# Attention of block 1: the values as loaded operand, two heads at a time, features on rows

## The chip, the cores and the metric

The kernel runs on one core of a Trainium2 chip. The metric is the device time of one execution in microseconds (us), as a median of several. The core has five engines with an instruction stream each: TensorE (PE in the profile; PEld is its weight loading), VectorE (DVE), ScalarE (ACT), GpSimd (POOL) and SyncE (SP, which here issues most DMAs). TensorE multiplies a loaded operand (weights, at most 128x128) by a moving one that streams by, and writes to PSUM; the other engines work on SBUF and, but for GpSimd here, on PSUM.

## The reference, cut to what matters

Two transformer blocks run on 512 tokens of 1024 features. The change lies in the sparse attention of block 1 (8 heads of 64 features in two groups of four that share keys and values). With 8 blocks of 64 keys and room for 16 chosen ones every causal block is chosen, and the window is as long as the sequence, so both fine branches are causal attention with a distance bias over different keys and values:

```python
def nsa_mixer(q, k_cmp, v_cmp, k_slc, v_slc, k_win, v_win, gate, ...):
    ...
    p_c = masked_softmax(s_c, dist_c >= 0)
    o_cmp = jnp.einsum('bgrsn,bngd->bsgrd', p_c.astype(vc.dtype), vc)
    ...
        pr = masked_softmax(s, (dist >= 0)[:, :, None])
        return jnp.einsum('bgrqk,bgqkd->bgrqd', pr.astype(vg.dtype), vg)
    ...
    gates = jax.nn.sigmoid(gate).reshape(B, S, G, R, 3)
    o = gates[..., 0:1] * o_cmp + gates[..., 1:2] * o_slc + gates[..., 2:3] * o_win
    return o.reshape(B, S, H * dv)

def first_block(x, p, ...):
        ...
        g_a, g_b = jnp.split(jax.nn.sigmoid(gmix), 2, axis=-1)
        mixed = (g_a * (ya @ w_a2d[i]) + g_b * (yb @ w_b2d[i])) @ w_o[i]
```

## The kernel before

Large products are made in a form of float32 with fewer bits (fp32r): each operand is split into a high half, rounded by a ScalarE copy, and a low half, which VectorE gets by subtraction, and three matmuls (`whi`, `wlo` are the halves of the weights) give one product. The weights come by SP's queue into three buffers `raw` and are split there. Some small products are made in plain float32, where the program's one matmul runs as two instructions.

The attention of block 1 is `nsa_tile(qt)` (L981) for the four query tiles of 128 tokens. Tile qt looks at W = 128(qt+1) keys. It first makes the compressed branch for all 8 heads (L985 to L1012). Then for branch `br` and head `h` it calls `attend` (L957): two matmuls make the scores (PSUM tile `sc`), one VectorE reduction adds the bias into the SBUF tile `P` and finds the extremum, ScalarE takes the exponential in place and sums it, TensorE transposes `P` 128 columns at a time (L968) into the PSUM tile `tp`, ScalarE (L229) and VectorE (L974) copy it in turn into `PT`, and plain float32 matmuls with the 128x128 pieces of `PT` as loaded operand and 64 columns of the values `VT` as moving one add up the output in `pv`, query tokens on rows. There are 64 such heads in all. `P` has three buffers, `PT` two, each PSUM tag two. After the 8 heads of a branch VectorE takes reciprocals of the sums, multiplies by the gate and adds the branch to `o0` (L1025 to L1029). At the end of the tile 4 transpositions bring `o0` to features on rows (`tr4`, L711), and it is split into `yb`.

TensorE has a filler beside this: `gmix` (L914), which makes the gates of the mixture, 16 chunks of 24 matmuls, and then `ya @ w_a2d`, 8 chunks of 12 (rows `mm<-u,whi` and `mm<-a,whi`, 512 columns each). `gmix.run(0.55 * (qt + 1))` per head releases so much of it. A scheduler that knows estimated durations then sets the order of the whole program, and every engine runs its instructions in that order. After the four tiles `gmix.flush()` (L1045) stands, and then the projection of `yb` (L1051). `scan_step` (L916) and `scan_out` (L948), ahead of the tiles, belong to the other mixer of the block; its states lie in `Sst`. Block 2 has an attention of its own by the same `attend` (L1304), which the change leaves.

Of the kernel before, what the change touches and what calls it, by code (L numbers as in the profile page):

```python
# [6 lines left out]
F32 = mybir.dt.float32  # L7
# [185 lines left out]
def body(tc, nc, A, dbg=None, upto=99):  # L193
# [13 lines left out]
    def sb(pool, shape, dt=F32, tag=None, bufs=1):  # L207
        if tag is None:
            nx[0] += 1
            return pool.tile(list(shape), dt, name=f"n{nx[0]}", bufs=bufs)  # L210
        return pool.tile(list(shape), dt, name=tag, tag=tag, bufs=bufs)

    def unit(tag, dt=F32):
        return sb(base, [128, 4, 512], dt, tag, {"u": 4, "a": 11}[tag])
# [41 lines left out]
    ident = cst  # L256
# [248 lines left out]
    gn05 = sb(pA, [128, 1])  # L505

    NG = A["gcst"].shape[1]
    gc0, gc = unit("a").rearrange("p a b -> p (a b)")[:, :NG], sb(pA, [128, NG], F32R)
    POOL.dma_start(gc0, A["gcst"])
    act(gc, gc0, AF.Copy)  # L510
    GR = {k: gc[:, a:b] for k, (a, b) in GCST.items()}
# [5 lines left out]


    U = {nm: unit("a") for nm in "kqv"}
    KV = unit("a")  # L520
    VT = KV[:, 2:4].rearrange("p a b -> p (a b)").rearrange("p (k c) -> p k c", k=4)
    Sst = [r4(KV[:, 0]), r4(KV[:, 1])]
    sm = sb(pA, [128, QT, 32])
    so = outs4(0, 288)
    tout(u, range(8), so, width=288, per=3, tail=3)
    for qt in range(QT):
        DVE.tensor_copy(sm[:, qt], so[qt][:, 256:])
        act(VT[:, qt], so[qt][:, :256], AF.Copy)
    beta, hb, az, gg, ngb = (sb(pA, [128, QT, 4]) for _ in range(5))
    gate = sb(pA, [128, QT, 24])  # L530
    tt(gg, sm[:, :, 4:8], bc(dtb[:, None, :], [128, QT, 4]), ALU.add)
# [74 lines left out]
            yield from fout_g(r, u)  # L606
            qsplit(r[0], QS[0][:, t], QS[1][:, t], 0.125 * 2.0 ** (t + 1), 0.125 * 2.0 ** (t + 5))

    ZF = sb(pA, [128, 4, 512])

    def z_gates():

# [300 lines left out]

    gmix = Fill(gates())  # L914

    def scan_step(c):  # L916
        Sc, Sn = Sst[c % 2], Sst[(c + 1) % 2]
        ut = r4(u0[:, c])
        if c:
            up = ps("sc", B4)  # L920
            for h in range(4):
                mm(up[:, h], r4(wT[:, c])[:, h], Sc[:, h])
            tt(ut, ut, up, ALU.add)
        if c < QT - 1:
            sp_ = ps("tp", B4)
            for h in range(4):
                mm(sp_[:, h], r4(kn[:, c])[:, h], ut[:, h])
            if c:
                tt(Sn, Sc, b4(glast[:, c]), ALU.mult, POOL)
                tt(Sn, Sn, sp_, ALU.add)  # L930
            else:
                DVE.tensor_copy(Sn, sp_)
        op_ = ps("pv", B4)
        for h in range(4):
            if c:
                mm(op_[:, h], r4(qdF[:, c])[:, h], Sc[:, h], start=True, stop=False)
            mm(op_[:, h], r4(qkT[:, c])[:, h], ut[:, h], start=c == 0, stop=True)
        jk = sb(p1, [128, 8, 64], F32, "o0", 2).rearrange("p (h a) d -> p h (a d)", h=4)
        act(jk, op_, AF.Square, scale=128.0 ** -0.5)
        ms = stat(4)  # L940
        DVE.tensor_reduce(ms, jk, axis=AX.X, op=ALU.add)
        tt(ms, ms, rq2[:, c], ALU.mult)
        ts(ms, ms, EPS, None, ALU.add)
        POOL.tensor_tensor(ms, ms, mhalf[:, :4], op=ALU.pow)
        tt(ms, ms, rqk[:, 1, c], ALU.mult)
        tt(ut, op_, b4(ms), ALU.mult)
# [34 lines left out]
    def nsa_tile(qt):  # L981
# [4 lines left out]
        for h in range(8):  # L986
            g, r = divmod(h, 4)
            mm(cs[:, h].rearrange("p a n -> p (a n)"), N["QS"][g][:, r, tok(qt)], N["kc"][:, g].rearrange("p a n -> p (a n)"))
        cp = sb(p1, [128, 2, 8, 32], F32, "cp", 1)
        m8, s8 = stat(8), stat(8)  # L990
        c0 = cp[:, 0]
        tt(c0, cs[:, :, 0], bc(C["bc"][:, None, 32 * qt:32 * qt + 32], [128, 8, 32]), ALU.add)
# [5 lines left out]
        DVE.tensor_reduce(s8, c0, axis=AX.X, op=ALU.add)  # L998
        DVE.reciprocal(s8, s8)
        stt(s8, s8, C["rowok"][:, qt:qt + 1], gq[:, :, 0], ALU.mult, ALU.mult)  # L1000
        b = ps("tp", [128, 2, 128])
        for g in range(2):
            PE.transpose(b[:, g], c0[:, 4 * g:4 * g + 4].rearrange("p r n -> p (r n)"), ident)
        c1 = cp[:, 1].rearrange("p a b -> p (a b)").rearrange("p (g q) -> p g q", g=2)
        act(c1, b, AF.Copy)
        oc = ps("tp", [128, 8, 64])
        for g in range(2):
            mm(oc[:, 4 * g:4 * g + 4].rearrange("p r d -> p (r d)"), c1[:, g], N["VB"][:, g].rearrange("p r d -> p (r d)"))
        o0 = sb(p1, [128, 8, 64], F32, "o0", 2)
        tt(o0, oc, b8(s8), ALU.mult)  # L1010

        nd = C["nd"][:, (3 - qt) * 128:]  # L1012
        for br in range(2):
            acc, sums = ps("pv", [128, 8, 64]), stat(8)
            for h in range(8):
                g, r = divmod(h, 4)

                def score(o):
                    mm(o, N["QS"][g][:, r, tok(qt)], N["K1"][:, 2 * br + g, :W], start=True, stop=False)
                    mm(o, N["QS"][g][:, r, tok(qt)], N["KL"][:, 2 * br + g, :W], start=False, stop=True)  # L1020

                gmix.run(0.55 * (qt + 1))
                attend(p1, score, W, qt, lambda k: VT[:, k, br * 128 + g * 64:br * 128 + g * 64 + 64], acc[:, h],
                       sums[:, h:h + 1], nd, 2.0 ** -(h + 1))
            DVE.reciprocal(sums, sums)  # L1025
            tt(sums, sums, gq[:, :, 1 + br], ALU.mult)
            o1 = sb(p1, [128, 8, 64], F32, "o1", 1)
            tt(o1, acc, b8(sums), ALU.mult)
            tt(o0, o0, o1, ALU.add)  # L1029
        show(f"yb{qt}", o0)  # L1030
        b = tr4(o0.rearrange("p (j h) d -> p j (h d)", j=4), None, "tp")
        split(yb.h[0][:, :, tok(qt)], yb.l[0][:, :, tok(qt)], b)

    gmix.run(5)
    for c in range(QT):
# [349 lines left out]
```

## Time and profile before

| | us |
|---|---|
| median of 3 runs (lowest to highest) | 1559.28 (1555.16 to 1561.36) |
| the profiled execution's own time | 1559.06 |
| its span, first to last instruction | 1557.2 |
| TensorE busy (share of the span) | 1508.4 (97%) |
| VectorE busy | 857.8 (55%) |
| ScalarE busy | 639.7 (41%) |
| GpSimd busy | 97.5 (6%) |
| mean granted TensorE clock | 0.989 |

The tiles of `nsa_tile` run from about 270 to 468 us of the span. Busy is the union of an engine's instructions; a busy TensorE is not one at its peak, since matmuls are pipelined and their ends are modelled. The granted clock is given as a share of 2.4 GHz, of which 0.5 is the lower level.

### The profile page before, as it was taken

To read this page: it belongs to the slowest core of one execution; us is meant where nothing else is said; L and a number is where in the kernel's file an instruction comes from. 1 tells how busy PE (TensorE), PEld (TensorE's weight loads), DVE (VectorE), ACT (ScalarE), POOL (GpSimd) and SP (SyncE) were. 2 spreads that over 40 slices of the span, in tenths; PEclk is the share of its full clock that TensorE was granted. 3 is DMA by queue.
4 is the path that set the end of the run, shared out by engine and by line. 5 is a ranking of instruction groups with operands and counts; after the bars stand their busy time and mean duration, and the time that the engine had idled before them with its cause. 6 is when DMAs were issued, how large, how long until landed. Compare 5 with 4: busy or idle time off the path is not lost.

```text
span 1557.2 us, 19391 instructions
## 1 busy us (share of the span) xinstructions
PE 1508.4 (97%) x7512; PEld 1268.7 (81%) x7512; DVE 857.8 (55%) x1422; ACT 639.7 (41%) x1165; POOL 97.5 (6%) x163
## 2 busy tenths in 40 slices
PE   7998999999999999999999999999999999999997
PEld 6886888888877888888888878888878888888886
DVE  5778754556647555666565376789844333333232
ACT  5443553345524344444455354255643222232122
POOL 2012001000000110000011010020110000000000
PEclk9999999999999999999999999999899999999999
DMA  6314211211044053333389551264341233323331
GB/s 212 95 54 149 68 55 55 68 41 41 1 162 149 30 163 95 96 95 101 115 318 353 207 177 41 84 227 136 108 163 41 95 98 103 97 95 95 95 96 67
DMA packets 49051, 176.80 MB, mean 114 GB/s; under 512 B 5688, under 2 KB 5688, under 8 KB 48960
## 3 DMA queue, kind: packets, MB, share of 16 engines
q1 hardware_dynamic: 39168, 140.13, 27.5%
q0 software_dynamic: 9792, 35.43, 6.6%
q8 instruction: 59, 0.97, 0.2%
q14 instruction: 32, 0.26, 0.0%
HBM read 161.89 MB, written 16.27 MB: 114 GB/s over the span
## 4 chain that ended last, share of the span: by engine, by line
PE 90%; DVE 4%; DMA 2%; ACT 2%; issue 1%; POOL 0%; SPq 0%; POOLq 0%; DVEq 0%; ACTq 0%
PE mm L241 35%; PE sc L241 18%; PE pv L241 18%; PE tp L241 17%; PE tp L968 2%; DMA raw<-W 1%; DVE a L232 1%; ACT a L229 1%; PE tp L467 1%; DMA x<-x 1%; DMA a<-low 0%; DVE n L238 0%; PE tp L711 0%; DVE o L232 0%; DVE P L963 0%
## 5 line engine op out<-in xcount | busy, mean ns | idle before, releaser
L232 DVE TENSOR_TENSOR wlo<-raw,whi 128x1024 fp32r<-128x1024 f32 (+1 forms) x194 | 236.8, 1220 | 322.1 <-ACT whi L229 321.5
L229 ACT ACTIVATE whi<-raw 128x1024 fp32r<-128x1024 f32 (+1 forms) x208 | 219.6, 1056 | 425.4 <-PE mm L241 117.0
L241 PE MATMUL mm<-a,whi 128*128 128x512 f32 x608 | 192.0, 394 | 1.1 <-ACT a L229 1.1
L241 PE MATMUL mm<-u,whi 128*128 128x512 f32 x544 | 175.9, 400 | 0.0
L241 PE MATMUL pv<-a,whi 128*128 128x512 f32 (+2 forms) x576 | 160.2, 362 | 1.8 <-ACT a L229 1.2
L241 PEld LDWEIGHTS mm<-a,whi 128*128 128x128 f32 x608 | 113.5, 189 | 24.4 <-ACT a L229 1.4
L241 PEld LDWEIGHTS pv<-a,whi 128*128 128x128 f32 x576 | 104.2, 189 | 18.9 <-ACT a L229 2.1
L241 PE MATMUL mm<-a,wlo 128*128 128x512 f32 x304 | 119.1, 392 | 0.0
L241 PEld LDWEIGHTS mm<-u,whi 128*128 128x128 f32 x544 | 101.3, 190 | 19.6
L241 PE MATMUL tp<-a,whi 128*128 128x512 f32 x368 | 113.8, 390 | 0.0
L241 PE MATMUL mm<-u,wlo 128*128 128x512 f32 x272 | 107.9, 397 | 0.0
L241 PE MATMUL sc<-a,whi 128*128 128x512 f32 x336 | 104.2, 390 | 0.0
L241 PE MATMUL pv<-a,wlo 128*128 128x512 f32 (+2 forms) x288 | 103.7, 361 | 0.0
L238 DVE SCALAR_TENSOR_TENSOR n<-n,n,n 128x511 f32<-128x511 f32 (+23 forms) x120 | 85.0, 733 | 4.8 <-ACT n L229 2.8
L241 PEld LDWEIGHTS tp<-a,whi 128*128 128x128 f32 x368 | 69.1, 188 | 14.3
L241 PE MATMUL sc<-a 128*128 128x128 f32 (+4 forms) x288 | 73.0, 352 | 3.1 <-DVE st L963 3.0
L241 PEld LDWEIGHTS sc<-a,whi 128*128 128x128 f32 x336 | 63.3, 188 | 13.0
L241 PEld LDWEIGHTS pv<-a,PT 128*128 128x128 f32 x480 | 65.3, 196 | 9.3 <-ACT PT L229 4.6
L241 PE MATMUL tp<-a,wlo 128*128 128x512 f32 x184 | 71.6, 389 | 0.0
L241 PE MATMUL pv<-a,PT 128*128 128x64 f32 x480 | 65.4, 272 | 4.3 <-ACT PT L229 3.2
L241 PEld LDWEIGHTS mm<-a,wlo 128*128 128x128 f32 x304 | 57.3, 188 | 11.7
L241 PE MATMUL sc<-a,wlo 128*128 128x512 f32 x168 | 65.4, 389 | 0.0
(351 smaller groups left out, 2732.1 us busy)
## 6 DMA issues: line engine op xcount, KB each, us to landing
raw<-W SPq DMA_DIRECT2D x234, 512.0 KB, 3.6
a<-W SPq DMA_DIRECT2D x22, 512.0 KB, 6.6
low<-a POOLq DMA_DIRECT2D x22, 512.0 KB, 6.7
wlo<-low POOLq DMA_DIRECT2D x14, 512.0 KB, 3.9
w<-rows POOLq DMA_DIRECT2D x7, 512.0 KB, 8.7
a<-low POOLq DMA_DIRECT2D x7, 512.0 KB, 4.7
bd<-bd POOLq DMA_DIRECT2D x8, 320.0 KB, 6.6
x<-x SPq DMA_DIRECT2D x4, 512.0 KB, 9.3
```

The costliest lines, as they stand in the source:

```text
L229: return ACT.activation(out, in_, f, **k)
L232: return (e or DVE).tensor_tensor(out, a, b, op=op)
L238: return DVE.scalar_tensor_tensor(out, a, s, b, op0=op0, op1=op1)
L241: return PE.matmul(out, lhsT=l, rhs=r, start=start, stop=stop, **k)
L467: PE.transpose(b[:, j, :], src[:, k * 128:(k + 1) * 128], ident)
L968: PE.transpose(b[:, k * 128:(k + 1) * 128], p_[:, k * 128:(k + 1) * 128], ident)
```

## The change

Numerators are divided by their sum and multiplied by the gate before they are transposed (GpSimd multiplies `P` by a factor per row that VectorE makes), and the transposed numerators of two heads stand side by side in `PT`, split into halves, for each head by a ScalarE copy and a VectorE subtraction. The values `VT` are kept as 64 high and 64 low columns, which are loaded together, and 256 columns of `PT` (2 heads by 128 tokens) stream by: the output has features on rows (64 of the high part of the values, 64 of the low part), two instructions per key tile, branch and pair of heads, both branches into the same PSUM tile. Four VectorE additions per group of heads bring the two parts into `y`, where the compressed branch, made in the same layout, already lies. The transposition at the end of a tile goes away. For space the scan's states move to buffers of `P`, the compressed branch's `cp` to the constants' buffer `gc`, and `PT` of branch 0 to the buffer of `ZF` (named `zp`); `PT` of either branch has one buffer. `attend` stays for block 2.

```diff
--- before.py
+++ after.py
@@ -505,7 +505,7 @@
     gn05 = sb(pA, [128, 1])
 
     NG = A["gcst"].shape[1]
-    gc0, gc = unit("a").rearrange("p a b -> p (a b)")[:, :NG], sb(pA, [128, NG], F32R)
+    gc0, gc = unit("a").rearrange("p a b -> p (a b)")[:, :NG], sb(pA, [128, NG], F32R, "gc")
     POOL.dma_start(gc0, A["gcst"])
     act(gc, gc0, AF.Copy)
     GR = {k: gc[:, a:b] for k, (a, b) in GCST.items()}
@@ -517,15 +517,15 @@
 
 
     U = {nm: unit("a") for nm in "kqv"}
-    KV = unit("a")
-    VT = KV[:, 2:4].rearrange("p a b -> p (a b)").rearrange("p (k c) -> p k c", k=4)
-    Sst = [r4(KV[:, 0]), r4(KV[:, 1])]
+
+    VT = unit("a", F32R).rearrange("p k (b d) -> p k b d", b=4)
     sm = sb(pA, [128, QT, 32])
     so = outs4(0, 288)
     tout(u, range(8), so, width=288, per=3, tail=3)
     for qt in range(QT):
         DVE.tensor_copy(sm[:, qt], so[qt][:, 256:])
-        act(VT[:, qt], so[qt][:, :256], AF.Copy)
+        v = so[qt][:, :256].rearrange("p (b d) -> p b d", b=4)
+        split(VT[:, qt, :, :64], VT[:, qt, :, 64:], v)
     beta, hb, az, gg, ngb = (sb(pA, [128, QT, 4]) for _ in range(5))
     gate = sb(pA, [128, QT, 24])
     tt(gg, sm[:, :, 4:8], bc(dtb[:, None, :], [128, QT, 4]), ALU.add)
@@ -606,7 +606,7 @@
             yield from fout_g(r, u)
             qsplit(r[0], QS[0][:, t], QS[1][:, t], 0.125 * 2.0 ** (t + 1), 0.125 * 2.0 ** (t + 5))
 
-    ZF = sb(pA, [128, 4, 512])
+    ZF = sb(pA, [128, 4, 512], F32R, "zp").bitcast(F32)
 
     def z_gates():
 
@@ -913,8 +913,11 @@
 
     gmix = Fill(gates())
 
+    state, NP = [None], 3
+
     def scan_step(c):
-        Sc, Sn = Sst[c % 2], Sst[(c + 1) % 2]
+        Sc, Sn = state[0], r4(sb(p1, [128, 512], F32, "P", NP)) if c < QT - 1 else None
+        state[0] = Sn
         ut = r4(u0[:, c])
         if c:
             up = ps("sc", B4)
@@ -986,7 +989,7 @@
         for h in range(8):
             g, r = divmod(h, 4)
             mm(cs[:, h].rearrange("p a n -> p (a n)"), N["QS"][g][:, r, tok(qt)], N["kc"][:, g].rearrange("p a n -> p (a n)"))
-        cp = sb(p1, [128, 2, 8, 32], F32, "cp", 1)
+        cp = sb(pA, [128, NG], F32R, "gc").bitcast(F32)[:, :512].rearrange("p (i h n) -> p i h n", i=2, h=8)
         m8, s8 = stat(8), stat(8)
         c0 = cp[:, 0]
         tt(c0, cs[:, :, 0], bc(C["bc"][:, None, 32 * qt:32 * qt + 32], [128, 8, 32]), ALU.add)
@@ -998,38 +1001,55 @@
         DVE.tensor_reduce(s8, c0, axis=AX.X, op=ALU.add)
         DVE.reciprocal(s8, s8)
         stt(s8, s8, C["rowok"][:, qt:qt + 1], gq[:, :, 0], ALU.mult, ALU.mult)
+        tt(c0, c0, bc(s8[:, :, None], [128, 8, 32]), ALU.mult)
         b = ps("tp", [128, 2, 128])
         for g in range(2):
             PE.transpose(b[:, g], c0[:, 4 * g:4 * g + 4].rearrange("p r n -> p (r n)"), ident)
         c1 = cp[:, 1].rearrange("p a b -> p (a b)").rearrange("p (g q) -> p g q", g=2)
         act(c1, b, AF.Copy)
-        oc = ps("tp", [128, 8, 64])
+        oc = ps("tp", B4)
+        for j in range(4):
+            g, i = divmod(j, 2)
+            mm(oc[:, j], N["VB"][:, g, 2 * i:2 * i + 2].rearrange("p r d -> p (r d)"), c1[:, g])
+
+        y = sb(p1, [128, 8, 64], F32, "o0", 2).rearrange("p (j a) d -> p j (a d)", j=4)
+        act(y, oc, AF.Copy)
+
+        nd = C["nd"][:, (3 - qt) * 128:]
         for g in range(2):
-            mm(oc[:, 4 * g:4 * g + 4].rearrange("p r d -> p (r d)"), c1[:, g], N["VB"][:, g].rearrange("p r d -> p (r d)"))
-        o0 = sb(p1, [128, 8, 64], F32, "o0", 2)
-        tt(o0, oc, b8(s8), ALU.mult)
-
-        nd = C["nd"][:, (3 - qt) * 128:]
-        for br in range(2):
-            acc, sums = ps("pv", [128, 8, 64]), stat(8)
-            for h in range(8):
-                g, r = divmod(h, 4)
-
-                def score(o):
-                    mm(o, N["QS"][g][:, r, tok(qt)], N["K1"][:, 2 * br + g, :W], start=True, stop=False)
-                    mm(o, N["QS"][g][:, r, tok(qt)], N["KL"][:, 2 * br + g, :W], start=False, stop=True)
-
-                gmix.run(0.55 * (qt + 1))
-                attend(p1, score, W, qt, lambda k: VT[:, k, br * 128 + g * 64:br * 128 + g * 64 + 64], acc[:, h],
-                       sums[:, h:h + 1], nd, 2.0 ** -(h + 1))
-            DVE.reciprocal(sums, sums)
-            tt(sums, sums, gq[:, :, 1 + br], ALU.mult)
-            o1 = sb(p1, [128, 8, 64], F32, "o1", 1)
-            tt(o1, acc, b8(sums), ALU.mult)
-            tt(o0, o0, o1, ALU.add)
-        show(f"yb{qt}", o0)
-        b = tr4(o0.rearrange("p (j h) d -> p j (h d)", j=4), None, "tp")
-        split(yb.h[0][:, :, tok(qt)], yb.l[0][:, :, tok(qt)], b)
+            acc = ps("pv", [128, 2, 2, 128])
+            for i in range(2):
+                for br in range(2):
+                    PT = (sb(p1, [128, 4, 512], F32R, "PT", 1) if br else sb(pA, [128, 4, 512], F32R, "zp"))
+                    PT = PT.rearrange("p a b -> p (a b)").rearrange("p (s k r q) -> p s k r q", s=2, k=4, r=2)
+                    for r in range(2):
+                        h = 4 * g + 2 * i + r
+                        gmix.run(0.55 * (qt + 1))
+                        sc = ps("sc")
+                        mm(sc[:, :W], N["QS"][g][:, 2 * i + r, tok(qt)], N["K1"][:, 2 * br + g, :W], start=True, stop=False)
+                        mm(sc[:, :W], N["QS"][g][:, 2 * i + r, tok(qt)], N["KL"][:, 2 * br + g, :W], start=False, stop=True)
+                        p_ = sb(p1, [128, 512], F32, "P", NP)[:, :W]
+                        mn, sm_ = stat(), stat()
+                        DVE.tensor_tensor_reduce(out=p_, in0=sc[:, :W], in1=nd, scale=-2.0 ** -(h + 1), scalar=3e38,
+                                                 op0=ALU.add, op1=ALU.min, accum_out=mn)
+                        act(p_, p_, AF.Exp, scale=-1.0, bias=mn, accum_out=sm_)
+                        DVE.reciprocal(sm_, sm_)
+                        tt(sm_, sm_, gq[:, h, 1 + br:2 + br], ALU.mult)
+                        tt(p_, p_, bc(sm_, [128, W]), ALU.mult, POOL)
+                        b = ps("tp", B4)
+                        for k in range(qt + 1):
+                            PE.transpose(b[:, k], p_[:, k * 128:(k + 1) * 128], ident)
+                        split(PT[:, 0, :qt + 1, r], PT[:, 1, :qt + 1, r], b[:, :qt + 1])
+                    for k in range(qt + 1):
+                        for s_ in range(2):
+                            mm(acc[:, i], VT[:, k, 2 * br + g], PT[:, s_, k], start=br + k + s_ == 0,
+                               stop=br == 1 and k == qt and s_ == 1)
+            for r in range(2):
+                yr = y[64 * r:64 * r + 64, 2 * g:2 * g + 2]
+                for part in (acc[0:64], acc[64:128]):
+                    tt(yr, part[:, :, r], yr, ALU.add)
+        show(f"yb{qt}", y)
+        split(yb.h[0][:, :, tok(qt)], yb.l[0][:, :, tok(qt)], y)
 
     gmix.run(5)
     for c in range(QT):
```

On TensorE, the end of the attention: the rows from the last of the filler (`mm<-a,wlo`) to the first matmul of the projection of `yb` (the last row). Names are output, then the moving and the loaded operand; `n_63` is the identity of the transpositions. Before:

```order
L241 MATMUL mm<-a,wlo 128x512
L241 MATMUL pv<-a,PT 128x64 x4
L968 MATMUL tp<-n_63,P 128x128 x2
L241 MATMUL pv<-a,PT 128x64 x4
L968 MATMUL tp<-n_63,P 128x128 x2
L241 MATMUL pv<-a,PT 128x64 x4
L711 MATMUL tp<-n_63,o_3660 128x128 x4
L241 MATMUL mm<-a,whi 128x512
```

And now. Between the last filler matmul and the first of these rows stand, left out here, the scores of three heads, the products of one pair (`pv<-zp,a`, 8) and the transpositions of one head:

```order
L241 MATMUL pv<-PT,a 128x256
L241 MATMUL sc<-a 128x512
L241 MATMUL sc<-n_1376,a 128x512
L241 MATMUL pv<-PT,a 128x256 x7
L1041 MATMUL tp<-n_63,P 128x128 x8
L241 MATMUL pv<-zp,a 128x256
L1041 MATMUL tp<-n_63,P 128x128 x4
L241 MATMUL pv<-zp,a 128x256 x7
L1041 MATMUL tp<-n_63,P 128x128 x4
L241 MATMUL pv<-PT,a 128x256 x8
L241 MATMUL mm<-a,whi 128x512
```

The scores of four heads, the transpositions of five and the products of four pairs (32 instructions) now stand behind the last filler matmul, where 12 products and 8 transpositions stood.

On VectorE, inside tile 2 (W = 384), where the filler is silent. `L963` is the reduction of the scores with its reading of the accumulator (now `L1033`). Before:

```order
L963 ISA P,st<-sc,n_199 128x384
L963 ISA st 128x1
L974 COPY PT<-tp 128x384
L963 ISA P,st<-sc,n_199 128x384
L963 ISA st 128x1
```

Now:

```order
L232 TENSOR_TENSOR zp<-tp,zp 128x3x128
L1033 ISA P,st<-sc,n_199 128x384
L1033 ISA st 128x1
L1036 RECIPROCAL st<-st 128x1
L232 TENSOR_TENSOR st<-st,n_336 128x1
L232 TENSOR_TENSOR PT<-tp,PT 128x3x128
L1036 RECIPROCAL st<-st 128x1
L1033 ISA P,st<-sc,n_199 128x384
L1033 ISA st 128x1
L232 TENSOR_TENSOR st<-st,n_336 128x1
```

Each head now brings five instructions to VectorE where two heads brought five: the low half stands where every second head had a copy, and a reciprocal and a product of 128x1 for each have come in between.

## Rows read from the trace of the kernel before

**Rows 1.** The page's chain that ended last, shares of the span by engine.
```profile
PE 90%; DVE 4%; DMA 2%; ACT 2%; issue 1%; POOL 0%; SPq 0%; POOLq 0%; DVEq 0%; ACTq 0%
```

**Rows 2.** Stretches: length, engines' busy us, then granted clock, DMA share, GB/s.
```profile
318.14:334.27 16.13, 13.56 (x85) 11.75 (x83) 12.14 (x47) 9.67 (x34) 0.00 (x0) 0.82 0.11 34
334.27:364.88 30.61, 30.61 (x172) 26.49 (x171) 10.40 (x31) 11.23 (x30) 0.00 (x0) 0.98 0.16 52
364.88:421.49 56.61, 51.77 (x400) 47.43 (x399) 41.91 (x120) 34.03 (x89) 0.00 (x0) 1.00 0.04 10
421.49:460.79 39.30, 39.30 (x198) 32.96 (x197) 14.33 (x24) 10.99 (x19) 3.25 (x6) 1.00 0.39 138
460.79:468.33 7.54, 4.02 (x34) 3.43 (x32) 4.50 (x6) 2.56 (x3) 0.00 (x0) 1.00 0.37 119
```

**Rows 3.** The chain of waits, 410 to 470 us: start, duration, what.
```profile
418.16 0.84 PE pv L241 x8
419.00 0.44 PE tp L968 x4
419.44 0.46 PE sc L241 x2
...
421.65 10.91 PE mm L241 x48
...
461.84 1.24 DVE wlo L232
...
463.10 3.62 DMA raw<-W
```

**Rows 4.** Timeline of TensorE near 346 us: start, duration, instruction.
```profile
346.15 0.28 PE L241 MATMUL sc<-n,a 128*128 128x256 f32 x1
346.27 0.28 PE L241 MATMUL sc<-a 128*128 128x256 f32 x1
```

**Rows 5.** VectorE's groups by shape, 270 to 462 us: total, mean ns.
```profile
L963 DVE CUSTOM_DVE_ANT_0 P<-sc,n 128x512 f32<-128x512 f32 x16 | 10.9, 683 | 3.6 <-PE sc L241 1.5 <-PE tp L968 1.1 <-ACT P L229 1.0
L963 DVE CUSTOM_DVE_ANT_0 P<-sc,n 128x384 f32<-128x384 f32 x16 | 8.7, 549 | 2.9 <-PE tp L968 1.5 <-ACT P L229 0.8 <-PE sc L241 0.7
...
L963 DVE DVE_READ_ACCUMULATOR2_ANT st<- 128x1 f32 x64 | 5.3, 83 | 0.0
...
L974 DVE COPY PT<-tp 128x384 f32<-128x384 f32 x8 | 4.5, 556 | 1.8 <-PE tp L968 1.8
...
L1025 DVE RECIPROCAL st<-st 128x8 f32<-128x8 f32 x8 | 1.6, 201 | 2.2 <-ACT P L229 2.2
```

**Rows 6.** VectorE's groups by shape, the whole span, two small shapes.
```profile
L232 DVE TENSOR_TENSOR a<-sc,dm 64x256 f32<-64x256 f32 x12 | 5.0, 420 | 0.7 <-PE sc L241 0.5
L238 DVE SCALAR_TENSOR_TENSOR st<-st 128x1 f32<-128x1 f32 x32 | 5.0, 156 | 29.3 <-ACT t L229 27.3 <-ACT at L229 1.9
```

**Rows 7.** ScalarE's groups by shape, 270 to 462 us.
```profile
L229 ACT ACTIVATION_READ_ACCUMULATOR P<-P,st 128x1 f32 x64 | 12.0, 188 | 0.0
...
L229 ACT ACTIVATE P<-P,st 128x384 f32<-128x384 f32 x16 | 9.8, 614 | 6.0 <-DVE st L963 5.9
...
L229 ACT ACTIVATE PT<-tp 128x384 f32<-128x384 f32 x8 | 3.9, 483 | 3.3 <-PE tp L968 3.3
```

**Rows 8.** GpSimd's groups by shape, the whole span, a product of 128x512.
```profile
L232 POOL TENSOR_TENSOR h<-a,n 128x512 f32<-128x512 f32 x4 | 4.3, 1069 | 3.6 <-DVE a L232 3.6
```

**Rows 9.** Timeline of GpSimd near 252 us (VectorE splits weights beside it).
```profile
252.32 1.95 POOL L232 TENSOR_TENSOR a<-a,n 128x512 f32<-128x512 f32 x1 [8.63 <-DVE a L932]
```

**Rows 10.** Timeline of VectorE near 241 us (GpSimd multiplies from 241.21 on).
```profile
241.26 1.53 DVE L232 TENSOR_TENSOR h<-a,n 128x512 f32<-128x512 f32 x1
```

**Rows 11.** Stretches of 4 us around the end of tile 0, as rows 2.
```profile
326.00:330.00 4.00, 2.19 (x14) 1.86 (x14) 3.96 (x14) 1.07 (x3) 0.00 (x0) 0.82 0.00 0
330.00:334.00 4.00, 3.83 (x14) 3.07 (x13) 1.53 (x6) 2.95 (x10) 0.00 (x0) 0.50 0.02 4
334.00:338.00 4.00, 4.00 (x18) 3.31 (x17) 0.68 (x3) 0.98 (x3) 0.00 (x0) 0.83 0.00 0
```

## Prediction

> **What bounds the kernel now.** I read the chain of waits first. Over the whole span 90% of the chain that ends last is TensorE [rows 1], so time is won only by shortening TensorE's work or filling its gaps, and lost wherever another engine becomes later than TensorE. Then I cut the touched part (block 1's attention, 270 to 468 us) at the places where the filler (the 512-column matmuls of the gates, which depend on nothing in the attention) starts and stops. [rows 2] gives the stretches after the first: A1 (318.14 to 334.27, no filler, end of query tile 0 and start of tile 1), A2 (filler of 4 gate chunks), A3 (364.88 to 421.49, no filler, end of tile 1, all of tile 2, start of tile 3), A4 (filler again) and the tail. A0, before them, is filled. The reader is to see that TensorE is busy for all of A2 and A4, while in A1, A3 and the tail it has 2.57, 4.84 and 3.52 us of gaps, with VectorE at 75%, 74% and 60%. So the filled stretches are bound by TensorE, and the unfilled ones by the interplay of score, reduction, exponential, transposition and copy per head, where VectorE is already close. The rest of the kernel is untouched but for one subtraction per key tile near 60 us, beside TensorE work, and counts nothing.
>
> **The change part by part.** *TensorE.* Before, each of the 160 products of 128 numerators by 64 values is two instructions, and 8 of them take 0.84 us [rows 3], 0.105 each: 320 x 0.105 = 33.6 us. After, 160 instructions of 256 columns do it. Matmuls of that width start 0.12 us apart (346.15 and 346.27 in [rows 4]), though those read other operands; 160 x 0.12 = 19.2, so 14.4 are saved. The 16 transposes at the ends of the tiles go as well, at 0.11 (4 in 0.44, [rows 3]): 1.8. In sum TensorE loses 16.2 us of work.
>
> *VectorE.* Per head the copy of the transposed numerators went to ScalarE or VectorE in turn. Now every head takes a ScalarE copy and a VectorE subtraction from the transposition's PSUM tile. No such subtraction stands in the trace; I take the PSUM copy of the same shape, 0.556 at 384 columns [rows 5], and 0.134 less or more per 128 columns (the step from 0.549 to 0.683 in [rows 5]). Further, per head, a reciprocal and a product on 128x1, at about 0.16 each ([rows 6] has 0.156 for such a shape; the 0.201 of 128x8 in [rows 5] is the upper bound), and per tile 8 additions of 64x256 at 0.420 [rows 6] where before two of 128x512 per branch stood. *GpSimd* multiplies the numerators by the gate over the sum, 1.07 us for 128x512 when alone [rows 8]. This stands between the exponential and the transposition: each head's chain grows by reciprocal, product, GpSimd multiply and crossings, some 1.5 us, which costs nothing as long as three P buffers hold enough heads in flight. The X loads now queue behind these multiplies on GpSimd's queue; they are wanted only after the gates' and yb's projections, whose weight loads alone take 3.62 us each [rows 3], so I cost that at nothing; without this cover it would be some us in the stage after.
>
> *Stretch by stretch* (the filler chunks in each stretch are the same before and after: the order shows 8, 4 and 2 gate chunks, then 8 of 12).
> A0: when the eighth chunk ends, after has 3 heads transposed, 6 scored and none multiplied by values, against 5, 8 and 3. That is 2 x 0.11 + 2 x 0.24 + 3 x 0.21 = 1.3 less: -1.3, deferred into A1.
> A1: VectorE now has 13 reductions with their reads (5.2), 13 low halves at 0.29 (3.7), 8 additions (3.4), 22 small ones (3.5), a compression step (3.3) and a weight split (1.2): 20.3. Such sums overstate: for the 120 instructions of A3 before I get 48.4 in the same way, and the union of their spans is 41.91 [rows 2], 0.86 of it. So 17.5 busy. Over 16.13 us this doesn't fit. At 95% dense it takes 18.4 (+2.3), at 80% 21.9 (+5.8, taken, since VectorE had 75% before with TensorE as a second limit), and with the small ones slower at 75% 24.8 (+8.6).
> A2: TensorE-bound. 96 matmuls at 0.227 (48 in 10.91, [rows 3]) are 21.8; compression 0.9, 14 transpositions 1.5, 5 pairs of scores 1.2, 8 products 1.0: 26.3 against 30.61: -4.3.
> A3: VectorE has 28 reductions (17.6), 29 low halves (15.5), 16 additions (6.7), 51 small ones (8.1), two compressions (6.7) and a split (1.2): 55.8, times 0.86 is 48.1. At 90% dense 53.4 (-3), at 80% 60.1 (+3.7, taken), at 75% with GpSimd in the way 68.5 (+12). ScalarE needs 0.614 + 0.188 + 0.483 = 1.29 us a head of 384 columns [rows 7], below VectorE's 1.5 (0.549 + 0.083 + 0.556 + 0.32), so it isn't the bound.
> A4: 144 filler matmuls 32.7, 24 products 2.9, 7 heads' transpositions 3.1, 4 pairs of scores at 0.46 [rows 3] 1.8: 40.5 against 39.30: +1.2.
> Tail: in the order before, 12 products and 8 transpositions are left after the last filler matmul, 2.1 us of TensorE work in 7.54. After, four heads are still to be scored, five to be transposed and 32 products to be made: 4 x 0.46 + 20 x 0.11 + 32 x 0.12 = 7.9 us of TensorE work, with nothing to fill. By the chain, three heads at VectorE's 512-column pace (0.683 + 0.083 + 0.69 + 0.32 = 1.8) are 5.3, and the last head's way is score 0.5, reduction 0.8, exponential 0.9, gate over sum 0.3, GpSimd 1.1, transposition 0.4, halves 1.3, products 1.0, additions 1.7, last halves 0.6: 8.6. With crossings, and the wait for a weight load of 3.62 and its split of 1.24 [rows 3] that now stand in the middle of this on VectorE, 16 to 18.5. I take 17: +9.5, with +6 if heads overlap at ScalarE's pace, and +11 at most.
> Net: -1.3 + 5.8 - 4.3 + 3.7 + 1.2 + 9.5 = +14.6 on the profiled run's 1559.06 (span 1557.2 and 1.9 around it; it stands 0.2 under the median, so nothing is rescaled): 1573.7, I say 1573. All low ends give -1.3 + 2.3 - 4.3 - 3 + 1.2 + 6 = +0.9, 1560; all high ends +27, 1586.
>
> *A rule against the change.* At 241.26 a VectorE product of 128x512 from two SBUF tensors took 1.53 us beside a GpSimd multiply [rows 10], where such a width takes about 0.69; a GpSimd multiply took 1.95 beside a weight split [rows 9] instead of 1.07 [rows 8]. Both directions enter the last rival below. The Trainium skill's GPSIMD Engine Reference, section Key points, says that GpSimd shares its SBUF interfaces with VectorE and contends with instructions there that have two SBUF inputs; the trace agrees. By the rule, the halves (one input in PSUM) would be spared and the 64 gate products not.
>
> **The rivals.** (a) The forecast: VectorE sets the unfilled stretches and the tail grows by what no longer stands under filler, 1573. (b) A wash: three P buffers let VectorE run dense and the low ends hold, 1560 to 1562. For it speaks that VectorE never waits for GpSimd's product directly; against it that its order alternates reductions and low halves of different heads, so a late head stops those behind it. (c) The other side: VectorE, ScalarE and GpSimd hide under TensorE and all of the 16.2 us is kept, 1543. It decides from the point where A3 ends within some 51 us, VectorE 94% dense, and the tail stays near 7.5; the 7.9 us of TensorE work left there speak against it, the full TensorE of A2 and A4 for a part. (d) Something slower on top. In [rows 11] TensorE was busy for 2.19 of 4 us, the granted clock fell to 0.82 and then 0.50 (the 1.2 GHz level) for 3.83 us of work, then 0.83. Against full clock that is about 0.4 + 1.9 + 0.7 = 3 us a time. A thinner TensorE in A1, at the tile changes in A3 and in the tail could meet this up to three times, +3 to +9; A3 now is at 1.00 throughout [rows 2], which speaks against it. Or contention: 25 gate products in A3, four in ten beside a GpSimd multiply, at 0.84 each, +8. Together with (a) some 1582 to 1590. The Trainium skill's TensorE: Matmul & The Clock Gate, Part 1, says that the clock is gated by how busy the array recently was; the rows agree.
>
> **How the numbers follow.** Chances: (a) 0.50, (b) 0.24, (c) 0.10, (d) 0.16. A measurement of this kernel tells some 0.5% from no change, 7.8 us: (c) is faster, (b) and a small part of (a) the same, the rest slower: 0.10, 0.28, 0.62. The range is 1556 to 1590: it leaves out (c) and the far ends. (a) alone has 1565 to 1582.
>
> **What would show it.** Right: the time from the start of A1 to the start of A2 longer by 2 to 9 us, A2 shorter by about 4, A3 with VectorE at 80% or more and the idle time of TensorE before transpositions released by GpSimd or VectorE, 16 us or so between the last gate matmul and yb's first projection. Wrong: products of 256 columns far from 0.12 us, low halves slower than 0.56 at 384 columns, a tail under 10 us, a clock under 0.9 in A3, or a difference outside 240 to 470 us.

## The result and the profile after

The changed kernel takes 1570.1 us (median of 5 runs, 1567.79 to 1571.69) against 1559.28; the ratio is 1.0073 with an interval of 1.006 to 1.0085. It is slower by 10.8 us, inside the range and on the side that was forecast, 2.9 under the forecast of 1573. One of e3's ten runs below took 1838.03 us at a granted clock of 0.77 and is left out where e3 is compared.

The same stretches, cut where the filler stops and starts (columns as in [rows 2]):

```profile
315.56:336.45 20.89, 16.73 (x70) 13.08 (x68) 17.59 (x83) 12.15 (x44) 4.41 (x11) 0.62 0.09 26
336.45:365.18 28.73, 28.73 (x138) 24.16 (x137) 12.99 (x40) 11.37 (x30) 6.06 (x10) 0.92 0.17 55
365.18:420.43 55.25, 43.46 (x260) 33.32 (x258) 49.80 (x178) 36.16 (x95) 23.03 (x28) 0.97 0.03 11
420.43:461.25 40.82, 40.82 (x204) 34.31 (x205) 23.37 (x48) 16.07 (x29) 6.82 (x7) 1.00 0.21 65
461.25:480.45 19.20, 11.59 (x61) 8.90 (x59) 12.85 (x30) 9.58 (x17) 7.25 (x10) 0.83 0.48 160
```

| stretch | before | forecast | after | difference |
|---|---|---|---|---|
| A0, from the filler block ahead of it (243.57, after 242.26) | 74.57 | -1.3 | 73.30 | -1.3 |
| A1, no filler | 16.13 | +5.8 | 20.89 | +4.8 |
| A2, filler | 30.61 | -4.3 | 28.73 | -1.9 |
| A3, no filler | 56.61 | +3.7 | 55.25 | -1.4 |
| A4, filler | 39.30 | +1.2 | 40.82 | +1.5 |
| tail | 7.54 | +9.5 | 19.20 | +11.7 |
| sum | | +14.6 | | +13.4 |

The profiled execution came 1.3 us earlier to this part than the one of before, and took 1.0 less behind it, so the spans differ by 11.1 (1568.3 and 1557.2). The loss is in A1, a little of it in A4 and, above all, in the tail.

The prices of the new operations, from VectorE's and then GpSimd's groups by line and shape between 270 and 478 us (total us, mean ns of one, idle time before):

```profile
L232 DVE TENSOR_TENSOR st<-st,n 128x1 f32<-128x1 f32 x64 | 14.6, 229 | 1.2
L232 DVE TENSOR_TENSOR o<-pv,o 64x256 f32<-64x256 f32 x29 | 12.2, 420 | 1.9 <-PE pv L241 1.3
L1036 DVE RECIPROCAL st<-st 128x1 f32<-128x1 f32 x64 | 10.1, 158 | 3.1 <-ACT P L229 2.3
L232 DVE TENSOR_TENSOR PT<-tp,PT 128x384 fp32r<-128x384 f32 x8 | 4.4, 552 | 0.0
```

```profile
L232 POOL TENSOR_TENSOR P<-P,st 128x512 f32<-128x512 f32 x16 | 16.5, 1040 | 49.4 <-DVE st L232 30.9 <-DVE st L1036 16.1 <-PE pv L241 2.4
L232 POOL TENSOR_TENSOR P<-P,st 128x384 f32<-128x384 f32 x16 | 13.7, 861 | 15.2 <-DVE st L1036 7.2 <-DVE st L232 4.9 <-ACT PT L229 2.1
```

Low halves, additions and reciprocals came as priced. The gate product took 229 ns on average instead of 160.

The chain of waits through the tail (start, duration, what), to be read against 461.84 and 463.10 in [rows 3]:

```profile
462.83 1.14 DVE wlo L232
463.97 0.45 DVE P L1033
...
464.66 0.59 DVE PT L232
465.25 0.60 DVE P L1033
...
466.09 1.05 POOL P L232
...
468.69 1.53 DVE a L232
...
470.24 3.47 DMA raw<-W
...
473.73 1.07 ACT a L229
...
474.82 1.23 DVE a L232
476.04 0.61 DVE PT L232
...
476.70 1.25 PE pv L241 x7
```

The `a` rows here are no numerators: they are splits of `w_o`'s weights for the stage behind the projection of `yb`. They stand in the in-order queues of ScalarE and VectorE ahead of the last heads' halves. VectorE's split at 468.69 frees the buffer into which the next chunk comes, ScalarE waits 3.47 us for that, and only behind ScalarE's and VectorE's split comes the last low half (476.04). From 468.69 to 476.04 the chain holds no step of a head. It is the path that ended last and not the price of the weights, for the last head's own steps ran beside it:

```profile
471.70 1.04 POOL L232 TENSOR_TENSOR P<-P,st 128x512 f32<-128x512 f32 x1 [2.58 <-DVE st L232]
```

```profile
474.69 0.58 ACT L229 ACTIVATE PT<-tp 128x512 fp32r<-128x512 f32 x1
```

ScalarE's copy (second fence) was done at 475.27, so the last low half waited some 0.7 us more for the split. Four additions and the last high half follow, up to 480.45.

### The profile page after: what moved, and what is told of

It reads as the page before. It is cut to its first block, busy times and chain, and to the rows that moved or that the text cites. A ratio compares the mean times of both kernels' runs of the same rounds, so it can differ in the third digit from the quotient of the medians.

```text
span 1568.3 us, 19433 instructions
## 1 busy us (share of the span) xinstructions
PE 1508.8 (96%) x7352; PEld 1259.5 (80%) x7352; DVE 891.9 (57%) x1586; ACT 654.6 (42%) x1201; POOL 144.1 (9%) x227
## 4 chain that ended last, share of the span: by engine, by line
PE 88%; DVE 6%; ACT 2%; issue 1%; DMA 1%; POOL 1%; SPq 0%; POOLq 0%; DVEq 0%; ACTq 0%
PE mm L241 35%; PE sc L241 18%; PE pv L241 16%; PE tp L241 16%; DVE a L232 1%; DVE P L1033 1%; ACT a L229 1%; DVE o L232 1%; PE tp L971 1%; PE tp L467 1%; PE tp L1041 1%; DMA raw<-W 0%; DMA x<-x 0%; PE tp L711 0%; DVE n L238 0%
## 5 line engine op out<-in xcount | busy, mean ns | idle before, releaser
L241 PE MATMUL sc<-a 128*128 128x512 f32 (+4 forms) x264 | 71.2, 362 | 4.1 <-DVE st L1033 3.1
L448 POOL TENSOR_TENSOR st<-st,n 128x1 f32<-128x1 f32 x32 | 19.3, 603 | 580.1 <-DVE st L238 580.1
L241 PEld LDWEIGHTS mm<-a,wlo 128*128 128x128 f32 x304 | 57.2, 188 | 11.7
L229 ACT ACTIVATE P<-P,st 128x128 f32<-128x128 f32 (+3 forms) x96 | 53.8, 562 | 20.8 <-DVE st L1033 15.5
```

Source lines behind the costliest of these rows:

```text
L229: return ACT.activation(out, in_, f, **k)
L241: return PE.matmul(out, lhsT=l, rhs=r, start=start, stop=stop, **k)
L448: POOL.tensor_tensor(r, r, mhalf[:, 0:1], op=ALU.pow)
```

## The experiments

A stretch is cut as above in each; times of single runs are given without an interval. The part behind the tail, which none of these edits but e10's touches, is up to 3.1 us longer in their profiled executions than in the changed kernel's, so totals of single runs say less than their stretches.

**Less work for VectorE.** e1 takes the normalisation out:

```diff
-                        DVE.reciprocal(sm_, sm_)
-                        tt(sm_, sm_, gq[:, h, 1 + br:2 + br], ALU.mult)
-                        tt(p_, p_, bc(sm_, [128, W]), ALU.mult, POOL)
```

> The changed kernel without the reciprocal, the gate product and GpSimd's multiply of each of the 64 heads (the numerators go to the transposition undivided, so the output lacks the division and the gate of both fine branches). It takes 64 x (0.158 + 0.229) = 24.8 us of instructions from VectorE and one engine from each head's chain. If VectorE's total load sets the unfilled stretches: A1 20.9 -> about 17, A3 55.3 -> about 48, tail 19.2 -> about 17, time 1555 to 1558. If the tail is set by what lost its cover and by the weight load of 3.5 us in the middle of it, A3 shrinks but the tail stays at 16 or more: 1558 to 1564. If the half clock of A1 (granted 0.62) is what costs there, A1 stays above 19.5.

One run took 1568.96, 1.1 less than the changed kernel. A1 19.22, A3 55.02, tail 20.37. Neither of the first two readings holds, and A1 is a little under the 19.5 of the third. VectorE was busy for 42.43 us in A3 instead of 49.80, and the stretch lasted as long. The rows say where it went (A3, then two pieces of 4 us out of it):

```profile
363.01:418.03 55.02, 47.14 (x263) 36.65 (x262) 42.43 (x122) 36.50 (x96) 0.00 (x0) 0.88 0.03 10
```

```profile
379.00:383.00 4.00, 3.32 (x15) 2.52 (x14) 0.95 (x3) 1.71 (x6) 0.00 (x0) 0.50 0.00 0
...
407.00:411.00 4.00, 2.85 (x9) 2.16 (x10) 2.07 (x5) 1.75 (x4) 0.00 (x0) 0.50 0.00 0
```

Both lie at the changes to tiles 2 and 3, where TensorE has little to do while VectorE makes the compressed branch: it was busy for 2.50 and 3.03 of the 4 us ahead of them. The granted clock was at 1.2 GHz there, and A3 as a whole at 0.88 instead of 0.97.

e2 takes the low halves out, with TensorE's work kept:

```diff
-                        split(PT[:, 0, :qt + 1, r], PT[:, 1, :qt + 1, r], b[:, :qt + 1])
+                        act(PT[:, 0, :qt + 1, r], b[:, :qt + 1], AF.Copy)
-                            mm(acc[:, i], VT[:, k, 2 * br + g], PT[:, s_, k], ...
+                            mm(acc[:, i], VT[:, k, 2 * br + g], PT[:, 0, k], ...
```

> The changed kernel without the low halves of the transposed numerators: VectorE's 64 subtractions are left out and the products read the high half twice, so TensorE's work is the same and VectorE loses 31 us of instructions. If VectorE's load sets the unfilled stretches: A1 20.9 -> about 17, A3 55.3 -> 45 to 48, tail 19.2 -> 16 or so, time 1553 to 1558. If the tail's missing cover is the main price, the tail stays at 15 or more and keeps most of the loss: 1558 to 1563. If the clock costs in A1, A1 stays above 19.5 with a clock under 0.7.

1560.14. A1 19.96 (granted 0.61), A3 49.93, tail 17.05. The low halves are worth 10 us, half of it in A3 (which stays over the 45 to 48 of the first reading) and 2.2 in the tail; most of the tail's growth stays without them. A1 hardly moved, as the reading by the clock had it.

**The clock.** e5 keeps TensorE busy in tile 0 with matmuls whose results are overwritten:

```diff
+                        for _ in range(2 if qt == 0 else 0):
+                            mm(sc, N["QS"][g][:, 2 * i + r, tok(qt)], N["K1"][:, 2 * br + g])
                         mm(sc[:, :W], ...
```

> The changed kernel with two more matmuls of 512 columns ahead of the scores of each of tile 0's 16 heads, into the same PSUM tile, which the scores then overwrite; some 20 of the 32 fall into A1, 4.6 us at full clock. If the half clock (0.62 granted in A1, from 320 to 340 us) is what lengthens A1, the clock stays near full, A1 goes from 20.9 to 16 to 19 and A2 starts at full clock (28.7 -> 26.5 to 27.5), although TensorE has more to do: 1564 to 1569 with the 2.8 us that A0 gains. If VectorE's 17.6 us of work set A1, it stays at 20.5 or more whatever the clock is: 1572 or more. If the clock falls all the same, A1 grows by 5 to 9 us.

1574.27; A0 grew by 4.7 (242.50 to 320.46). A1 took 19.12 and A2 28.15. The projection of `yb` begins only 1.1 us later than in the changed kernel; 3.1 us of the longer time lie behind the tail. The clock was at 1.00 up to 335 us, but two reductions fewer were left for A1 (11 instead of 13). Within it VectorE was as dense as at half clock:

```profile
320.46:339.58 19.12, 15.93 (x88) 12.85 (x87) 16.03 (x74) 11.80 (x40) 5.23 (x11) 0.89 0.09 29
```

16.03 of 19.12 is 84%, and 17.59 of 20.89 in the changed kernel is 84% as well. So full clock alone did not make A1 denser; what it took off goes with the two heads. e9 does e2 and e5 together (diffs as there).

> e2_no_low (no low halves of the numerators) together with the two extra matmuls per head of tile 0 that the scores overwrite. Either one alone shortened A1 by 1 to 2 us. If VectorE's work and the half clock of TensorE bound A1 side by side, both together bring A1 to 14 to 16.5 us and the clock there above 0.85; if neither does and it is the order of the heads, A1 stays at 18 or more. Time 1560 to 1566 (the extra matmuls cost A0 some 3 to 5 us).

1562.1, A1 18.11 with a clock of 0.95: below the three others (20.89, 19.96, 19.12), but not the 14 to 16.5 that two bounds side by side would have given. VectorE was busy for 13.88 us of it, 77%, and in the kernel before for 12.14 of 16.13, 75%, with as many heads left (11): at about the same share, the difference is its work. What holds it at that share stays open; the longer way of each head is a candidate that no run here isolates.

e11 repeats e1 with TensorE kept busy at the tile changes:

```diff
-        b = ps("tp", [128, 2, 128])
+        bw = ps("tp")
+        b = bw[:, :256].rearrange("p (a b) -> p a b", a=2)
+        for _ in range(14 if qt > 1 else 0):
+            mm(bw, N["QS"][0][:, 0, tok(qt)], N["K1"][:, 0])
```

> e1_no_norm (no division and gate of the numerators) with 14 more matmuls of 512 columns ahead of the compressed branch's transposition in tiles 2 and 3, into the PSUM tile that the transposition then overwrites. In e1_no_norm A3 fell to half clock at both tile changes (379 to 387 and 407 to 415 us) and lasted 55.0 as with VectorE's 7 us more. If the clock took that gain back, A3 has 0.95 or more here and lasts 50 to 54 although TensorE has 6.4 us more to do; if the order of the heads sets A3, 55 or more.

1563.51, 5.5 less than e1 with more work:

```profile
363.00:414.23 51.23, 46.57 (x296) 38.42 (x294) 43.49 (x125) 35.94 (x96) 0.00 (x0) 1.00 0.04 11
```

A3 is at full clock and 3.8 us shorter than in e1 with 28 matmuls more. So the clock had taken back what the lighter VectorE gave. The tail fell to 17.01 as well, at 0.92 instead of 0.74. Between e2 and e9 it hardly moved with the clock (the tails of e2, then e9):

```profile
454.50:471.55 17.05, 10.85 (x65) 8.83 (x64) 10.17 (x25) 9.87 (x18) 8.31 (x11) 0.86 0.47 151
```

```profile
455.50:472.37 16.87, 9.90 (x66) 7.90 (x64) 10.18 (x25) 10.00 (x18) 8.40 (x11) 1.00 0.48 165
```

**Buffers.** e6 leaves two buffers of P:

```diff
-    state, NP = [None], 3
+    state, NP = [None], 2
```

> The changed kernel with two buffers of P for the numerators instead of three. If the longer way of a head (reciprocal, product, GpSimd, crossings) is hidden by the heads in flight, fewer of them open it: A3 55.3 -> 63 or more, A1 and the tail longer, 1580 or more. If the sum of VectorE's instructions sets the unfilled stretches, A3 stays within 2 us and the time within 1568 to 1574.

1594.24, with A1 24.16, A3 71.49 and a tail of 25.45. VectorE had little more to do than with three (52.58 us for 49.80):

```profile
367.70:439.19 71.49, 55.41 (x262) 39.85 (x261) 52.58 (x177) 35.97 (x95) 21.91 (x27) 0.83 0.03 8
```

Its share falls from 90% to 74%. Its reductions waited 12.2 us for the transpositions that free a buffer of `P`, against 4.5 in the changed kernel. The third buffer is what lets VectorE run dense over GpSimd's step and the crossings. The granted clock was lower as well (0.83 for 0.97), which this run doesn't separate.

**The tail.** e3 releases the filler later in the changed kernel, e4 in the kernel before, by the same line:

```diff
-                        gmix.run(0.55 * (qt + 1))
+                        gmix.run(0.40 * (qt + 1))
```

> The changed kernel with the filler released at 0.40 instead of 0.55 us per head and key tile, so that the last chunks of it stand beside and behind the last heads; all work is the same. If the tail's missing cover is the main price: the stretch from the last head's scores to the projection of yb has TensorE busy, 8 to 11 us are won back, 1559 to 1563. If VectorE's load sets the time, the filler only moves and A4 becomes an unfilled stretch: 1567 to 1572.

> The kernel before with the same 0.40. Its tail has 3.5 us of gaps and its other unfilled stretches 7.4: if cover at the end is what counts, it wins at most 3.5 us, 1555.5 to 1559; if it makes no difference, 1559.

e3 took 1558.96 (median of nine; 1559.41 of all ten), ratio to the kernel before 1.0003 (0.9992 to 1.0014): some 11 us won back with all the work in place. From the filler's start behind A3 to the projection of `yb` TensorE has no gap:

```profile
418.85:467.56 48.71, 48.71 (x267) 41.66 (x266) 31.75 (x74) 22.54 (x43) 16.27 (x18) 1.00 0.31 102
```

48.71 stands against 60.02 (40.82 and 19.20) in the changed kernel and 46.84 before. The heads' work on VectorE in it is the same (10 reductions, 13 low halves, 8 additions); three weight splits fewer fall into it. What differs is that the last heads have matmuls beside them. A1 and A3 stayed as they were (21.57 and 55.14). e4 took 1553.65, ratio 0.9969 (0.9956 to 0.9981): 4.3 less than the kernel before, whose runs beside it took 1557.97, slightly more than the 3.5 us of gaps in its tail had allowed for. So with both tails under cover the change still costs some 5 us, and the cover accounts for about half of the 10.8.

e10 takes `w_o`'s splits out of the tail, by loading the seven chunks unsplit over GpSimd's queue:

```diff
...
+                if len(W) < 8 and a is NOSPLIT[0] and p:
+                    W[hf, k // 2] = p()
+                    for half in W[hf, k // 2]:
+                        POOL.dma_start(half, A["W"][wi[0]])
+                    wi[0] += 1
...
```

> The changed kernel in which the seven weight chunks of w_o that are loaded after the first one come from memory as they are into both halves, over GpSimd's queue, without ScalarE's and VectorE's split (so the output is wrong by the second half). It takes the two splits out of the tail that stand ahead of the last low halves on ScalarE and VectorE and wait there for a transfer of 3.5 us. If that wait is what makes the tail 19.2 instead of the 17 of the sum: 13 to 16. If the tail is the heads' own chain: 17.5 or more. Time 1563 to 1568, or 1568 to 1571.

1574.49, tail 19.62. The tail as a whole settles nothing, since the edit put another wait in the place of the one it took away. GpSimd's queue (first fence) and VectorE's (second) at that place:

```profile
465.82 2.12 POOL L427 DMA_DIRECT2D a<-W  x4 [1.67 <-PE sc L241]
467.93 2.07 POOL L232 TENSOR_TENSOR P<-P,st 128x512 f32<-128x512 f32 x2
```

```profile
467.31 2.71 DVE L232 TENSOR_TENSOR st<-st,n 128x1 f32<-128x1 f32 x1
```

The multiplies of two heads, whose factors VectorE had made by 466.6, waited for four DMA issues, and the third head's gate product took 2.71 us, up to the end of both multiplies. From the last reduction on, where nothing of this is left, it was 11.3 us to the projection (469.95 to 481.26), against 12.5 in the changed kernel (467.99 to 480.45). In these 11.3 us the chain holds steps of heads alone, among them:

```profile
472.74 1.86 PE pv L241 x7
474.61 0.87 PE tp L1049 x4
...
476.87 1.88 PE pv L241 x7
```

So without any weight in its way the last head takes nearly as long, but at a lower clock, 0.50 for 0.74 in the changed kernel's 12.5:

```profile
469.95:481.26 11.31, 7.57 (x29) 5.92 (x29) 5.40 (x14) 3.58 (x7) 6.36 (x11) 0.50 1.07 406
```

The edit also changes the stage behind: 3.5 of the 4.4 us by which the run is longer than the changed kernel lie there.

e12 gives TensorE more to do in the tail, to hold its clock:

```diff
+                        for _ in range(5 if qt == 3 and h > 5 else 0):
+                            mm(b.rearrange("p a b -> p (a b)"), N["QS"][g][:, 2 * i + r, tok(qt)], N["K1"][:, 2 * br + g])
```

> The changed kernel with five more matmuls of 512 columns ahead of the transpositions of each of the last four heads, into the PSUM tile that the transpositions then overwrite: 20 x 0.227 = 4.5 us of work for TensorE inside the tail, the rest in the same order. In the tail of the changed kernel the clock stood at 0.71 and 0.56 in the last 12 us, and products, transpositions and the first projection's matmuls ran at half speed there. If that is part of the price, the clock stays above 0.9, the tail goes from 19.2 to 17 to 18.3 and the projection behind it starts at full clock: 1566 to 1568.5. If the tail waits on VectorE, ScalarE and the transfer alone, the added work changes nothing or costs up to 4 us: 1570 to 1574.

1574.54, ratio 1.0113 (1.0096 to 1.013), the tail 22.40 at a clock of 0.91. Slower by some 4 us, as the second reading had it. In the profiled execution (1572.71) the tail starts 1.7 us earlier than in the changed kernel and ends 1.5 later. Its chain:

```profile
465.85 1.07 ACT a L229
...
466.94 1.71 DVE a L232
...
468.67 3.63 DMA raw<-W
...
472.33 1.06 ACT a L229
...
473.42 1.24 DVE a L232
...
474.67 5.63 DMA raw<-W
...
480.32 1.58 ACT a L229 x2
```

No step of a head but the last high half is in it. Each transfer waits for the split that frees its buffer, and the last high half of `yb` stands behind the third of these splits in ScalarE's queue. But the heads' steps beside it were longer too (TensorE's queue):

```profile
473.53 1.84 PE L241 MATMUL tp<-a 128*128 128x512 f32 x5
```

Five of the added matmuls took 1.84 us ahead of the last transposition, and VectorE's last additions, 1.77 us from 478.36 on, ended at 480.13, so the split holds up the last high half (481.28) by 1.2 us. The matmuls that were to raise the clock stand in the heads' way themselves, and the run gives the tail's clock no price.

**Later still.** e7 and e8 release less ahead of the tiles as well, in the changed kernel and in the kernel before:

```diff
-    gmix.run(5)
+    gmix.run(1)
...
-        gmix.run(5)
+        gmix.run(1)
...
-                gmix.run(0.55 * (qt + 1))
+                gmix.run(0.4 * (qt + 1))
```

> The changed kernel with the filler released later still: 1 instead of 5 us at each of the five places ahead of the tiles and 0.40 per head and key tile, so that 4 or so gate chunks leave the time before tile 0's end for all of tile 1, and chunks are left to the end. If TensorE's gaps in unfilled stretches and the tail are the price, tile 1 is filled throughout, A3 shrinks to tile 2: 1552 to 1557. If VectorE's total sets the time: 1558 to 1561, as with 0.40 alone.

> The kernel before with the same later release. If the gaps are the price: 1548 to 1553, 4 us or so under the changed kernel with the same release, since its VectorE has 34 us less to do; if TensorE's saving of 16 us counts as soon as all is filled, it is 4 us or more above that one.

1553.02 (0.9968, 0.9958 to 0.9977) and 1548.03 (0.9941, 0.9926 to 0.9955). Tile 1 is filled in both, and the stretches without filler are the rest of tile 0 and tile 2. The changed kernel's (with its last stretch, up to the projection of `yb`), then the other's:

```profile
297.61:319.19 21.58, 19.15 (x80) 15.36 (x79) 17.39 (x84) 12.27 (x45) 5.89 (x13) 0.60 0.08 26
...
375.70:412.47 36.77, 29.11 (x186) 22.45 (x184) 34.57 (x115) 26.45 (x66) 15.23 (x18) 1.00 0.05 16
412.47:464.93 52.46, 48.81 (x267) 41.71 (x265) 34.43 (x76) 23.55 (x43) 15.37 (x18) 1.00 0.33 112
```

```profile
295.95:312.47 16.52, 13.64 (x93) 11.64 (x91) 12.26 (x51) 10.88 (x38) 0.00 (x0) 0.90 0.10 33
...
373.69:417.11 43.42, 41.47 (x326) 38.60 (x325) 31.61 (x86) 27.07 (x67) 0.00 (x0) 1.00 0.04 14
```

e8 beats both kernels, by 9.7 us against before, with three numbers of the filler's release changed and the products left as they were. The change still costs 5.0 us here. Tile 0 costs it 5.1, tile 2 gives 6.7 back (its cuts don't fall on the same head in both, so this is no clean price of a head). Its last steps are not all under cover: 3.65 us of gaps on TensorE are left ahead of the projection, where the kernel before has none. The rest was not taken apart.

## Why the prediction was right, and where its steps were off

**The direction and the main term held.** The filled stretches were bound by TensorE and the unfilled ones mostly by VectorE's queue (busy for 90% of A3, 84% of A1), so that 16 us less of TensorE work did not count where it was taken away. The largest term was the tail, and e3 shows that its cause is the missing cover: some 11 us come back when filler stands there, of which the kernel before gains 4.3 by the same line (e4). That the sum came so near (+13.4 for +14.6) is in part luck: A3 was forecast 5.1 us too long, A2 and the tail 2.4 and 2.2 too short.

**The tail was undersized**, +9.5 taken and +11 at most, against +11.7. The step that failed is the last head's way, which I had priced at full clock and with one weight load and split in its middle: from its reduction on the sum has 8.1 us (8.6 less the scores' 0.5), and it took 12.5. Two paths ran side by side there. One is the weights: the chain has 1.14 + 1.53 + 3.47 + 1.07 + 1.23 = 8.4 of the tail's 19.2 us of them, 7.3 behind the last reduction. The other is the head's own way at a low clock: e10 took 11.3 for it without weights, at 0.50, where seven products took 1.86 and 1.88 us instead of 0.83 and the transposition 0.87 instead of 0.44, which is 2.5 of the 3.2 us over the sum. Taking off either one gave little: 1.2 us without the weights (e10), 0.2 from e2 to e9 with the clock raised from 0.86 to 1.00, where the chain holds the weights again (transfers of 3.48 and 3.46 us with their splits). From e1 to e11, without normalisation, the tail fell by 3.4 with the clock (0.74 to 0.92). No run of the changed kernel takes off both, so how they share the tail's excess stays open. The kernel before had such a round of weights already, at 461.84 and 463.10 in [rows 3]; the chain in its tail holds little else.

**A3 was oversized**, +3.7 against -1.4, within its bounds of -3 to +12. (60.1 less 56.61 is 3.5, a slip of 0.2.) Its sum was good (48.1 forecast, 49.80 measured); the density was the error. I took 80% for VectorE because it had 74% before; it ran at 90%. e6 shows why it could: with three buffers of P its reductions waited only 4.5 us in A3 for one to come free.

**A2 gave 1.9 instead of 4.3.** Its sum of 26.3 was for full clock, and A2 began at half clock, with 0.92 in the mean: 0.92 x 28.73 is 26.4. The rows of before had shown this at the same place (0.83 in [rows 11]), and I had left it to the last rival alone.

**A1 came near**, +4.8 for +5.8, with 17.59 us of VectorE work where 17.5 was forecast. The reason was only half of it. A lighter VectorE (e1, e2) takes 1.7 and 0.9 us off, more clock none beyond the heads that went with it (e5), both together 2.8 (e9).

**Prices.** 7 products took 0.83 us (462.29 to 463.12), 0.119 each for the 0.12 that I took from other operands. A0 and A4 came within 0.3 us. The gate product was 0.07 dearer than priced, 4.4 us in all 64, and the ten of A3's 25 that I had put beside a GpSimd multiply did not cost 0.84 each: of its 28 one took 0.91, five 0.41 to 0.59 and the others 0.27 or less. The X loads behind GpSimd's multiplies cost nothing that shows, the part behind the tail being 1.0 shorter.

**The rivals.** A wash would have needed a tail of 13.5; a gain, that A1 and the tail had not grown. The clock, rival (d), came true in A1 and the start of A2, where it was at 0.50 for some 16 us. Its price shows in A2 (2.3 us, 0.08 of 28.73), which TensorE bounds; in A1, where VectorE's share was 84% at either clock (e5), it doesn't. The Trainium skill's TensorE: Matmul & The Clock Gate, Part 1, has the clock follow the array's recent activity. e11 agrees: with matmuls whose results nobody reads the granted clock of A3 rose from 0.88 to 1.00, and the kernel took 5.5 us less than e1.

## What to carry to other kernels

A saving on the busiest engine counts only where that engine sets the pace; so cut the stage where filler starts and stops, and sum each piece with its own limit. Ask first what stands behind the last filler matmul: releasing filler later took 9.7 us off the kernel before, and the changed arithmetic, with its tail uncovered, had added 10.8. And a share of the chain that ended last is no price: 8.4 us of weight splits and transfers stood on it here, and with them gone the way was 1.2 us shorter.

## What the runs showed of the hardware

A product of 128x1 on VectorE, 0.15 to 0.16 us by itself, took 0.91 us beside a GpSimd multiply (VectorE at 410.31, GpSimd from 410.17 on; first and second fence), and 2.71 in e10, where it ended with the second of two multiplies. There it had begun 0.62 us ahead of the first of them, while GpSimd issued DMAs, though two such products earlier beside these issues (466.15 and 466.41) took 0.16; what it waited for until the multiply began isn't shown. The additions with one operand in PSUM beside the next multiply kept their 0.42 to 0.43 (two in 0.86 at 411.32).

```profile
410.31 0.91 DVE L232 TENSOR_TENSOR st<-st,n 128x1 f32<-128x1 f32 x1
411.15 0.15 DVE L1036 RECIPROCAL st<-st 128x1 f32<-128x1 f32 x1
411.32 0.86 DVE L232 TENSOR_TENSOR o<-pv,o 64x256 f32<-64x256 f32 x2
```

```profile
410.17 1.04 POOL L232 TENSOR_TENSOR P<-P,st 128x512 f32<-128x512 f32 x1 [3.36 <-DVE st L1036]
411.39 1.04 POOL L232 TENSOR_TENSOR P<-P,st 128x512 f32<-128x512 f32 x1 [0.18 <-DVE st L1036]
```

Both products ended when GpSimd's multiply did, which looks like a wait for its instruction rather than a slower rate; for longer VectorE instructions the two weren't told apart. The Trainium skill's GPSIMD Engine Reference, section Key points, has VectorE's instructions with two SBUF inputs contend with GpSimd for its SBUF interfaces, and the trace agrees: the product has both operands there, the additions have one.
